# Attention core: value products on two column halves, and the softmax division moved behind them

## The chip, the cores and the metric

The kernel runs on one core of one Trainium2 chip. The metric is the time of one execution on the device, in microseconds (us). Engines are called as in the profile: PE is TensorE (matrix products), PEld its weight loads, DVE is VectorE, ACT is ScalarE, POOL is GpSimd, SP is SyncE, which issues the loads. PSUM is the memory that PE writes, in eight banks of 128 x 512 fp32 numbers.

## The reference

A two-layer backbone block: 512 tokens of width 1024 and 256 context tokens. Each layer is a half-step SwiGLU network, a token mixer and another half-step SwiGLU network, each with modulation and normalisation. The first layer's mixer is attention, and in it lies the change: 16 query heads of 64 on 4 key heads (four query heads share keys and values), blocks of 128 queries, each with the block's own keys, its neighbours' and all 256 context keys, and a logit ("sink") per head that only adds to the softmax's sum.

```
def block(bi):
    ...
    s_win = jnp.where(valid, s_win, NEG_INF)
    s_ctx = jnp.einsum('bqhgd,bkhd->bhgqk', q_b, kc, preferred_element_type=jnp.float32)
    sinks = jnp.broadcast_to(sink_logit, s_ctx.shape[:-1] + (1,))
    p = jax.nn.softmax(jnp.concatenate([s_win, s_ctx, sinks], axis=-1), axis=-1).astype(v.dtype)
    o = (jnp.einsum('bhgqk,bkhd->bqhgd', p[..., :SPAN], v_b)
         + jnp.einsum('bhgqk,bkhd->bqhgd', p[..., SPAN:SPAN + C_], vc))
    return o
```

## The kernel before

The large products (the two networks, the projections) run on PE with operands split into a rounded part and a rest (`wh`, `wl` for weights; three products instead of one). Weights come in tiles of 128 x 1024: loaded as `wr`, for some multiplied by a gate's row (`wr<-wr,gr`, on DVE), rounded on ACT (`wh`), and the rest taken on DVE (`wl<-wr,wh`).

The change lies in `attention`. Keys, values and queries are projected first (`group`, `kv_post`, `q_post`). Then follows the core: 16 steps, one per key head g and block b, in which four query heads (`GRP`) are handled at once. Blocks 0 and 3 have four key tiles of 128 (scores 512 wide, "narrow" below), blocks 1 and 2 have five (640 wide, "wide").

`scores` of a step: PE makes the scores of each head (s); DVE adds the mask, writes them to the tile p and takes the row's minimum of the negated scores (nm, in one or two instructions per head); ACT exponentiates p in place with the row's sum (sum) beside it. es is the exponential of the sink logit. At the end DVE adds es to sum, takes the reciprocal and scales p by it.

`weights_turned` of a step: PE turns the four p tiles into PSUM banks pt, one bank per key tile (16 or 20 turns), and ACT copies the banks to pT.

`values` of a step: one product per key tile, V as the stationary operand, the four heads' pT side by side as 512 columns. V holds each head's 64 columns twice, so o has the same values in rows 0 to 63 and 64 to 127; two ACT copies take the even heads from the upper half and the odd ones from the lower half into oT, which the output projection reads.

The loop over the steps writes the core out by hand: in step n stand `weights_turned` of n, `scores` of n + 2, in steps 3 to 6 a turn of queries (`q_flip`, qt), and `values` of n. In steps 2 to 5 DVE then splits queries (`q_parts`), in step 0 it adds a bias to the last ones (qb), and POOL rotates them (ra). In steps 7 to 11 one tile of the output projection's weights is prepared: wr at the step's start, wh and wl ahead of `values`. All engines but SP keep this order in the core (`pin`). PSUM tiles are taken from eight banks in turn.

Of the kernel before, what the change touches and what calls it, by code (L numbers as in the profile page):

```python
# [10 lines left out]
F32 = mybir.dt.float32  # L11
F32R = mybir.dt.float32r
AF = mybir.ActivationFunctionType
ALU = mybir.AluOpType

P = 128
# [13 lines left out]
KVH = 4  # L30
GRP = HEADS // KVH
HD = 64
# [11 lines left out]
HEAD_TURN = 2  # L44
HEAD_PE = 1
SLOTS = 42
EVAC_DVE = ()
CORE_FETCH = 7
CORE_TILES = 5
MOD_LAG = 3  # L50
# [52 lines left out]
class Emitter:  # L103
# [33 lines left out]
    def mm(self, out, lhsT, rhs, start, stop):  # L137
        self.nc.tensor.matmul(out, lhsT, rhs, start=start, stop=stop)
# [739 lines left out]
    def attention(self, w_kv, w_q, w_ao, h1, ch, rest):  # L878
        nc = self.nc
        ins = self.ins  # L880
        sync = nc.sync
        mm = self.mm
# [13 lines left out]
        V = []  # L896

        def kv_post(tp, ps):
            V.append(self.slot([P, 2, KVH, 2 * HD], F32, "V"))
            kv = self.slot([P, 2, 512], F32, "kvb")  # L900
            for tt in range(2):
                nc.vector.tensor_tensor(kv[:, tt], ps[:, tt * 512 : (tt + 1) * 512], bkv, ALU.add)
            kks = []
            for tt in range(2):
                t = 2 * tp + tt
                kr = kv[:, tt, :256]
                if t < NT:
                    kr = self.rope(kr, tabs[:, 0, t], tabs[:, 1, t], KVH, nc.vector)
                kk2 = self.slot([P, 2, KVH, 2, HD], F32, "kk2")
                k4 = kr.rearrange("p (h d) -> p h d", d=HD)  # L910
                for r in range(2):
                    nc.scalar.copy(kk2[:, 0, :, r].bitcast(F32R), k4)
                for r in range(2):
                    nc.vector.tensor_tensor(kk2[:, 1, :, r], k4, kk2[:, 0, :, r], ALU.subtract)
                kks.append(kk2)
            for tt in range(2):
                v4 = kv[:, tt, 256:512].rearrange("p (h d) -> p h d", d=HD).unsqueeze(2)
                nc.scalar.copy(
                    V[tp][:, tt].rearrange("p h (r d) -> p h r d", r=2), v4.broadcast_to([P, KVH, 2, HD])
                )  # L920
            return tp, kks

        def kv_flip(tp, kks, tt):
# [44 lines left out]
        def q_flip(tp, i, qb, q2s, tt):  # L968
            flip = self.bank2(nm="qt")
            for j in range(8):  # L970
                self.turn(flip[:, j * P : (j + 1) * P], q2s[tt][:, j].rearrange("p r d -> p (r d)"))
            q = self.slot([P, 8, P], F32R, "Q")
            for h in range(2):
                src = flip[:, h * BANK : (h + 1) * BANK].rearrange("p (j q) -> p j q", q=P)
                nc.scalar.copy(q[:, 4 * h : 4 * h + 4], src)
            Q[2 * tp + tt, i] = q
# [44 lines left out]
        sink = self.const([P, HEADS], F32, "sink")  # L1021
# [5 lines left out]
        oT = []  # L1027

        def scores(g, b):
            lo_t, hi_t = max(b - 1, 0), min(b + 1, NT - 1)  # L1030
            nw = (hi_t - lo_t + 1) * P
            win = [KX[g][:, part, lo_t * P : lo_t * P + nw] for part in range(2)]
            cx = [KC_[g // 2][:, g % 2, part] for part in range(2)]
            w_t = list(range(lo_t, hi_t + 1))
            c_t = list(range(NT, NT + NCT))
            segs = [(0, CTX, cx), (CTX, nw, win)] if b == NT - 1 else [(0, nw, win), (nw, CTX, cx)]
            keys = c_t + w_t if b == NT - 1 else w_t + c_t
            total = nw + CTX
            m0 = {0: 384, NT - 1: 0}.get(b, 256)
            cuts = [0, total] if total <= BANK else [0, nw, total]  # L1040
            part, nm, sm, es = (self.small([P, GRP], x) for x in ("part", "nm", "sum", "es"))
            s_l = [self.slot([P, total], F32, "p") for _ in range(GRP)]

            def expo(j):
                hd = g * GRP + j
                nc.scalar.activation(
                    s_l[j], s_l[j], AF.Exp, bias=nm[:, j : j + 1], scale=-1.0, accum_out=sm[:, j : j + 1]
                )
                if j % 2 == 1:
                    pair = slice(j - 1, j + 1)  # L1050
                    nc.vector.tensor_tensor(es[:, pair], sink[:, hd - 1 : hd + 1], nm[:, pair], ALU.add)
                    nc.scalar.activation(es[:, pair], es[:, pair], AF.Exp)

            for j in range(GRP):
                hd = g * GRP + j
                q = Q[b, hd // 8][:, hd % 8]
                least = nsink[:, hd : hd + 1]
                for c0, c1 in zip(cuts, cuts[1:]):
                    ps = self.bank("s")
                    for off, n, kp in segs:  # L1060
                        if c0 <= off < c1:
                            o = ps[:, off - c0 : off - c0 + n]
                            mm(o, q, kp[0], start=True, stop=False)
                            mm(o, q, kp[1], start=False, stop=True)
                    to = nm if c1 == total else part
                    nc.vector.tensor_tensor_reduce(
                        out=s_l[j][:, c0:c1], in0=ps[:, : c1 - c0], in1=mask[:, m0 + c0 : m0 + c1], scale=-1.0,
                        scalar=least, op0=ALU.add, op1=ALU.min, accum_out=to[:, j : j + 1],
                    )
                    least = to[:, j : j + 1]  # L1070
                if j > 0:
                    expo(j - 1)
            expo(GRP - 1)
            for j in range(0, GRP, 2):
                pair = slice(j, j + 2)
                nc.vector.tensor_tensor(sm[:, pair], sm[:, pair], es[:, pair], ALU.add)
                nc.vector.reciprocal(sm[:, pair], sm[:, pair])
                for i in range(j, j + 2):
                    nc.vector.tensor_scalar(s_l[i], s_l[i], sm[:, i : i + 1], None, ALU.mult)
            return g, b, keys, s_l  # L1080

        def weights_turned(g, b, keys, s_l):
            nk = len(keys)
            banks = [self.bank("pt") for _ in range(nk)]
            for i in range(nk):
                for j in range(GRP):
                    self.turn(banks[i][:, j * P : (j + 1) * P], s_l[j][:, i * P : (i + 1) * P])
            pT = []
            for i in range(nk):
                if i % 2 == 0:  # L1090
                    sb = self.slot([P, 2, 512], F32, "pT")
                src = banks[i]
                if i in EVAC_DVE:
                    nc.vector.tensor_copy(sb[:, i % 2], src)
                else:
                    nc.scalar.copy(sb[:, i % 2], src)
                pT.append(sb[:, i % 2])
            return g, b, keys, pT

        def values(g, b, keys, pT):  # L1100
            nk = len(keys)
            o = self.bank("o")
            for i, kt in enumerate(keys):
                mm(o, V[kt // 2][:, kt % 2, g], pT[i], start=(i == 0), stop=(i == nk - 1))
            tok = slice(b * P, (b + 1) * P)
            for r in range(2):
                rs = slice(r * HD, (r + 1) * HD)
                src = o[rs].rearrange("p (c r q) -> p c r q", c=2, r=2)[:, :, r]
                nc.scalar.copy(oT[g][rs, :, tok], src)

        steps = [(g, b) for g in range(KVH) for b in range(NT)]
        oT.append(self.slot([P, 2, SEQ], F32, "oT"))
# [2 lines left out]
        due = [scores(*steps[0])]  # L1115
        ps1 = group(1, w_q[1], between=lambda: due.append(scores(*steps[1])))
        q01 = q_bias(0, 1, ps0)
        for n, (g, b) in enumerate(steps):
            fetch = n >= CORE_FETCH and self.n_split < w_ao + CORE_TILES
            if fetch:  # L1120
                self.gate_next()
            t = weights_turned(*due.pop(0))
            if b == 0 and g > 0:
                oT.append(self.slot([P, 2, SEQ], F32, "oT"))
            if n + 2 < len(steps):
                due.append(scores(*steps[n + 2]))
            if Q_TURN <= n < Q_TURN + 4:
                q_flip(*(q01 if n < Q_TURN + 2 else q11), (n - Q_TURN) % 2)
            if fetch:
                self.weights(self.n_split, ahead=0)  # L1130
            values(*t)
            if n == 0:
                q11 = q_bias(1, 1, ps1)
                for i in range(4):
                    q_rope(*(q01 if i < 2 else q11), i % 2, nc.gpsimd)
            if Q_TURN - 1 <= n < Q_TURN + 3:
                q_parts(*(q01 if n < Q_TURN + 1 else q11), (n + 1 - Q_TURN) % 2)
# [205 lines left out]
```

## Time and profile before

| | |
|---|---|
| median of three runs | 2040.0 us (2038.52 to 2041.05) |
| the profiled execution | 2039.18 us, span 2037.3 us |
| PE busy | 2003.1 us, 98% of the span |
| DVE, ACT, POOL busy | 1324.4, 714.4, 50.5 us |
| granted TensorE clock | 0.998 of full speed |

Rows of groups read: line, engine, operation, out<-in by the program's names with buffer numbers left out, partitions x elements, count, then busy time in us and mean ns of one, and behind the second bar the engine's idle time just before them and who ended it. Nearly all lines are L70, a helper's, so groups are told apart by names. A product of fp32 tiles (o) leaves two records for each product of the program. Rows of the timeline read: start, duration, engine, operation. A duration includes the instruction's latency, so where instructions follow one another the distance between starts is what one costs.

### The profile page before, as it was taken

The numbers are of one execution on the slowest core, as the hardware profiler recorded it, in microseconds if no ns is written. First come the engines' busy times: TensorE is split into PE (matmuls) and PEld (weight loads), VectorE is DVE, ScalarE is ACT, GpSimd is POOL, SyncE is SP. The second block draws the span as 40 slices with busy tenths as digits, with TensorE's granted clock in tenths as the row PEclk, the third lists the DMA queues.
The fourth block names the chain that finished last, engine by engine and source line by source line (L and its number), as shares of the span: only waits on it lengthen the run. The fifth ranks groups of instructions, "written<-read, shape, count | busy, mean of one in ns | idle before, by whom it ended". The sixth has DMA issues, their size and how long they took to land.

```text
span 2037.3 us, 25228 instructions
## 1 busy us (share of the span) xinstructions
PE 2003.1 (98%) x9990; PEld 1683.6 (83%) x9990; DVE 1324.4 (65%) x1888; ACT 714.4 (35%) x1090; POOL 50.5 (2%) x56
## 2 busy tenths in 40 slices
PE   6999999999999999999999999999999999999998
PEld 5788888899888776888888889888888988888887
DVE  7659986598756887666657646665675882322854
ACT  3322233443634688422224323221332642222420
POOL 2000000000000300000000000000000000000000
PEclk9999999999999999999999999999999999999999
DMA  9656543387712002265543416454342223322321
GB/s 366 229 196 205 189 133 134 115 295 283 260 65 72 1 32 93 104 217 191 192 155 114 138 47 250 176 207 145 114 144 74 104 83 108 99 93 83 124 73 42
DMA packets 81910, 292.56 MB, mean 144 GB/s; under 512 B 9856, under 2 KB 10112, under 8 KB 81792
## 3 DMA queue, kind: packets, MB, share of 16 engines
q1 hardware_dynamic: 81792, 290.96, 41.4%
q8 instruction: 78, 1.28, 0.3%
q14 instruction: 40, 0.33, 0.0%
HBM read 288.83 MB, written 2.10 MB: 143 GB/s over the span
## 4 chain that ended last, share of the span: by engine, by line
PE 94%; DVE 4%; issue 0%; ACT 0%; DMA 0%; SPq 0%; DVEq 0%
PE up L70 52%; PE y L70 31%; PE qkv L70 4%; PE o L70 2%; DVE p L70 1%; DVE acc L70 1%; PE s L70 1%; PE pt L70 1%; PE tp L70 1%; PE f L70 1%; PE ab L70 0%; PE qt L70 0%; DVE wl L70 0%; DMA wr<-in_wi_head_dram 0%; PE gp L70 0%
## 5 line engine op out<-in xcount | busy, mean ns | idle before, releaser
L70 DVE TENSOR_TENSOR wl<-wr,wh 128x1024 fp32r<-128x1024 f32 x356 | 426.3, 1220 | 105.0 <-ACT wh L70 68.0
L70 ACT CAST wh<-wr 128x1024 fp32r<-128x1024 f32 (+1 forms) x364 | 367.3, 1046 | 191.7 <-PE y L70 99.7
L70 PE MATMUL up<-hh,wh 128*128 128x512 f32 (+1 forms) x1152 | 429.4, 373 | 0.0
L70 PE MATMUL up<-hl,wh 128*128 128x512 f32 (+1 forms) x1152 | 428.0, 372 | 0.0
L70 PE MATMUL up<-hh,wl 128*128 128x512 f32 (+1 forms) x1152 | 427.8, 371 | 0.0
L70 ACT ACTIVATE sg<-up 128x512 f32<-128x512 f32 (+1 forms) x110 | 61.2, 556 | 715.4 <-PE up L70 715.4
L70 PE MATMUL y<-wh,ul 128*128 128x512 f32 x920 | 302.5, 390 | 3.5 <-DVE ul L70 3.4
L70 PE MATMUL y<-wh,uh 128*128 128x512 f32 x920 | 303.2, 391 | 0.0
L70 PE MATMUL y<-wl,uh 128*128 128x512 f32 x920 | 302.3, 390 | 0.0
L70 DVE TENSOR_TENSOR u<-up,sg 128x512 f32<-128x512 f32 (+1 forms) x110 | 70.1, 637 | 354.1 <-PE up L70 353.8
L70 PEld LDWEIGHTS up<-hl,wh 128*128 128x128 f32 x1152 | 217.0, 188 | 37.6
L70 PEld LDWEIGHTS up<-hh,wl 128*128 128x128 f32 x1152 | 217.1, 188 | 37.1
L70 PEld LDWEIGHTS up<-hh,wh 128*128 128x128 f32 x1152 | 217.1, 188 | 36.9
L70 PEld LDWEIGHTS y<-wh,ul 128*128 128x128 f32 x920 | 173.1, 188 | 40.4 <-DVE ul L70 4.4
L70 PEld LDWEIGHTS y<-wh,uh 128*128 128x128 f32 x920 | 173.1, 188 | 35.9 <-ACT uh L70 0.4
L70 PEld LDWEIGHTS y<-wl,uh 128*128 128x128 f32 x920 | 173.1, 188 | 35.7
L70 DVE SCALAR_TENSOR_TENSOR acc<-mr,silu_c,acc 128x1024 f32<-128x1024 f32 x147 | 186.2, 1281 | 1.4
L70 DVE TENSOR_TENSOR wr<-wr,gr 128x1024 f32<-128x1024 f32 x104 | 124.8, 1221 | 29.4 <-DMA wr<-in_wo_dram 20.6
L70 PE MATMUL up<-h0h,wh 128*128 128x512 f32 x352 | 139.6, 397 | 3.3 <-ACT h0h L70 3.3
L70 PE MATMUL up<-h0h,wl 128*128 128x512 f32 x352 | 138.4, 393 | 0.0
L70 PE MATMUL up<-h0l,wh 128*128 128x512 f32 x352 | 138.2, 393 | 0.0
L70 DVE SCALAR_TENSOR_TENSOR x<-x,y 128x512 f32<-128x512 f32 x48 | 32.7, 682 | 105.3 <-PE y L70 105.3
(162 smaller groups left out, 2291.8 us busy)
## 6 DMA issues: line engine op xcount, KB each, us to landing
wr<-in_wi_dram SPq DMA_DIRECT2D x213, 512.0 KB, 4.5
mr<-in_mod_w_dram SPq DMA_DIRECT2D x144, 512.0 KB, 4.2
wr<-in_wo_dram SPq DMA_DIRECT2D x110, 512.0 KB, 3.6
m<-in_mod_head_dram SPq DMA_DIRECT2D x16, 512.0 KB, 8.2
wr<-in_wqkv_dram SPq DMA_DIRECT2D x12, 512.0 KB, 3.8
wr<-in_attn_wo_dram SPq DMA_DIRECT2D x8, 512.0 KB, 3.4
wr<-in_fourier_wo_dram SPq DMA_DIRECT2D x8, 512.0 KB, 3.6
wr<-in_wi_head_dram SPq DMA_DIRECT2D x8, 448.0 KB, 9.2
```

What stands on the lines that cost most here:

```text
L70: ins = f(*args, **kw)
```

## The change

V is stored once per head (64 columns). Each value product becomes two, for the even heads into rows 0 to 63 of o and for the odd ones into rows 64 to 127, with 256 columns each. p is no longer scaled. The four sums of a step get their reciprocals in one instruction that also spreads each over 64 elements (rs, 128 x 256); PE turns rs in two turns into a bank rr; ACT copies rr into oT's place, and DVE multiplies o by it there. es is made by one pair of instructions instead of two. The first pT bank of a step is copied by DVE instead of ACT (`EVAC_DVE`).

```diff
-EVAC_DVE = ()
+EVAC_DVE = (0,)
...
-            V.append(self.slot([P, 2, KVH, 2 * HD], F32, "V"))
+            V.append(self.slot([P, 2, KVH, HD], F32, "V"))
...
-                if j % 2 == 1:
-                    pair = slice(j - 1, j + 1)
-                    nc.vector.tensor_tensor(es[:, pair], sink[:, hd - 1 : hd + 1], nm[:, pair], ALU.add)
-                    nc.scalar.activation(es[:, pair], es[:, pair], AF.Exp)
...
+            nc.vector.tensor_tensor(es, sink[:, g * GRP : (g + 1) * GRP], nm, ALU.add)
             expo(GRP - 1)
-            for j in range(0, GRP, 2):
-                pair = slice(j, j + 2)
-                nc.vector.tensor_tensor(sm[:, pair], sm[:, pair], es[:, pair], ALU.add)
-                nc.vector.reciprocal(sm[:, pair], sm[:, pair])
-                for i in range(j, j + 2):
-                    nc.vector.tensor_scalar(s_l[i], s_l[i], sm[:, i : i + 1], None, ALU.mult)
-            return g, b, keys, s_l
+            nc.scalar.activation(es, es, AF.Exp)
+            return g, b, keys, s_l, sm, es
...
+            nc.vector.tensor_tensor(sm, sm, es, ALU.add)
+            rs = self.pool.tile([P, GRP, HD], F32, tag="rs", name=self.name("rs"), bufs=2)
+            nc.vector.reciprocal(rs, sm.unsqueeze(2).broadcast_to([P, GRP, HD]))
             nk = len(keys)
...
+            rows = self.bank("rr")
+            for c in range(2):
+                self.turn(rows[:, c * P : (c + 1) * P], rs[:, 2 * c : 2 * c + 2].rearrange("p r d -> p (r d)"))
             pT = []
...
+            nc.scalar.copy(oT[g][:, :, b * P : (b + 1) * P], rows[:, : 2 * P].rearrange("p (c q) -> p c q", c=2))
             return g, b, keys, pT
...
-            o = self.bank("o")
+            o = self.bank("o")[:, : 2 * P].rearrange("p (c q) -> p c q", c=2)
             for i, kt in enumerate(keys):
-                mm(o, V[kt // 2][:, kt % 2, g], pT[i], start=(i == 0), stop=(i == nk - 1))
+                heads = pT[i].rearrange("p (c r q) -> p c r q", c=2, r=2)
+                for r in range(2):
+                    mm(
+                        o[r * HD : (r + 1) * HD], V[kt // 2][:, kt % 2, g], heads[:, :, r],
+                        start=(i == 0), stop=(i == nk - 1),
+                    )
             tok = slice(b * P, (b + 1) * P)
-            for r in range(2):
-                rs = slice(r * HD, (r + 1) * HD)
-                src = o[rs].rearrange("p (c r q) -> p c r q", c=2, r=2)[:, :, r]
-                nc.scalar.copy(oT[g][rs, :, tok], src)
+            nc.vector.tensor_tensor(oT[g][:, :, tok], o, oT[g][:, :, tok], ALU.mult)
```

The order on DVE around the weight fetch of step 7, before: es of the last head pair, then the two halves of sums, reciprocals and scalings, then the fetch's two instructions, then the next scores' first mask (ISA).

```order
 L70 TENSOR_TENSOR es_6536<-sink,nm_6534 128x2
 L70 TENSOR_TENSOR sum_6535<-sum_6535,es_6536 128x2
 L70 RECIPROCAL sum_6535<-sum_6535 128x2
 L70 TENSOR_SCALAR p_6537<-p_6537,sum_6535 128x640
 L70 TENSOR_SCALAR p_6538<-p_6538,sum_6535 128x640
 L70 TENSOR_TENSOR sum_6535<-sum_6535,es_6536 128x2
 L70 RECIPROCAL sum_6535<-sum_6535 128x2
 L70 TENSOR_SCALAR p_6539<-p_6539,sum_6535 128x640
 L70 TENSOR_SCALAR p_6540<-p_6540,sum_6535 128x640
 L70 TENSOR_TENSOR wl_6592<-wr_5505,wh_6591 128x1024
 L70 TENSOR_TENSOR wr_5517<-wr_5517,gr_4995 128x1024
 L70 ISA p_6634,part_6630<-s_6638,mask_5555,nsink 128x384
```

The same place after the change:

```order
 L70 TENSOR_TENSOR es_6527<-sink,nm_6525 128x4
 L70 TENSOR_TENSOR wl_6573<-wr_5505,wh_6572 128x1024
 L70 TENSOR_TENSOR oT_6175<-o_6576,oT_6175 128x2x128
 L70 TENSOR_TENSOR wr_5517<-wr_5517,gr_4995 128x1024
 L70 TENSOR_TENSOR sum_6429<-sum_6429,es_6430 128x4
 L70 RECIPROCAL rs_6589<-sum_6429 128x256
 L70 COPY pT_6614<-pt_6591 128x512
 L70 ISA p_6625,part_6621<-s_6629,mask_5555,nsink 128x384
```

wl now follows es directly, the product with o and the gate multiply stand between it and sum, and sum and reciprocal are those of the step before, ahead of the eviction and the next masks.

On PE, the end of step 0 and the start of step 1, before: the last scores, the value products of step 0 (the number behind a row counts the program's products), the first turns of step 1.

```order
 L70 MATMUL s_5857<-K_843_5010,Q_5598 128x384 x2
 L70 MATMUL s_5861<-KC_847_5014,Q_5598 128x256 x2
 L70 MATMUL o_5877<-pT_5815,V_5066 128x512 x2
 L70 MATMUL o_5877<-pT_5818,V_5323 128x512 x2
 L70 MATMUL pt_5907<-ident,p_5716 128x128
```

After the change, the same value products, and then the end of step 1's turns:

```order
 L70 MATMUL s_5842<-K_843_5010,Q_5598 128x384 x2
 L70 MATMUL s_5846<-KC_847_5014,Q_5598 128x256 x2
 L70 MATMUL o_5854<-pT_5801,V_5066 64x256 x4
 L70 MATMUL o_5854<-pT_5804,V_5323 64x256 x4
 L70 MATMUL pt_5890<-ident,p_5706 128x128
...
 L70 MATMUL pt_5894<-ident,p_5709 128x128
 L70 MATMUL rr_5915<-ident,rs_5888 128x128 x2
 L70 MATMUL s_5935<-KC_847_5014,Q_5635 128x256 x2
```

There are twice as many products of half the columns, and two turns of rs stand between the turns of p and the next scores. In steps 10 and 11 two gate multiplies of the output projection's weights come to stand between DVE's sum and reciprocal.

More of the change, by code (lines that the diff above doesn't have):

```diff
@@ L916, in kv_post @@
             for tt in range(2):
[L917 to L920, printed above, removed]
+                nc.scalar.copy(V[tp][:, tt], kv[:, tt, 256:512].rearrange("p (h d) -> p h d", d=HD))
             return tp, kks
@@ L1044, in expo @@
             def expo(j):
-                hd = g * GRP + j
                 nc.scalar.activation(
@@ L1072, in scores, with weights_turned @@
                     expo(j - 1)
+            nc.vector.tensor_tensor(es, sink[:, g * GRP : (g + 1) * GRP], nm, ALU.add)
             expo(GRP - 1)
-            for j in range(0, GRP, 2):
-                pair = slice(j, j + 2)
-                nc.vector.tensor_tensor(sm[:, pair], sm[:, pair], es[:, pair], ALU.add)
-                nc.vector.reciprocal(sm[:, pair], sm[:, pair])
-                for i in range(j, j + 2):
-                    nc.vector.tensor_scalar(s_l[i], s_l[i], sm[:, i : i + 1], None, ALU.mult)
-            return g, b, keys, s_l
-        def weights_turned(g, b, keys, s_l):
+            nc.scalar.activation(es, es, AF.Exp)
+            return g, b, keys, s_l, sm, es
+        def weights_turned(g, b, keys, s_l, sm, es):
+            nc.vector.tensor_tensor(sm, sm, es, ALU.add)
+            rs = self.pool.tile([P, GRP, HD], F32, tag="rs", name=self.name("rs"), bufs=2)
+            nc.vector.reciprocal(rs, sm.unsqueeze(2).broadcast_to([P, GRP, HD]))
             nk = len(keys)
@@ L1121, in attention @@
                 self.gate_next()
-            t = weights_turned(*due.pop(0))
             if b == 0 and g > 0:
                 oT.append(self.slot([P, 2, SEQ], F32, "oT"))
+            t = weights_turned(*due.pop(0))
             if n + 2 < len(steps):
```

## The prediction

> **What bounds the kernel now.** I read the page first, of it the chain that ended last.
>
> ```profile
> PE 94%; DVE 4%; issue 0%; ACT 0%; DMA 0%; SPq 0%; DVEq 0%
> ```
>
> TensorE is the bound almost everywhere, so time won or lost on TensorE's path inside the attention core arrives at the end unchanged. The core runs from the first turn of softmax weights (pt) to the last value product (o). The timeline of PE gives both ends, the table by stage what is busy between (behind the length stand the busy times of PE, PEld, DVE, ACT and POOL with their counts, then the granted clock).
>
> ```profile
> 676.28 1.91 PE L70 MATMUL pt<-ident,p 128*128 128x128 f32 x16
> ...
> 806.62 3.60 PE L70 MATMUL o<-pT,V 128*128 128x512 f32 x8
> ```
>
> ```profile
> 676.00:811.00 135.00, 131.12 (x694) 92.67 (x693) 111.97 (x338) 106.81 (x259) 16.05 (x16) 1.00 0.12 40
> ```
>
> The core takes 810.22 - 676.28 = 133.9 us at full clock. PE is busy for 131 of 135 us and DVE for 112: a change that makes PE lighter meets DVE soon. The chain in order of time gives the lengths of PE's parts, the by-form groups a product record's mean duration.
>
> ```profile
> 690.60 4.29 PE o L70 x10
> 694.89 2.18 PE pt L70 x20
> 697.08 1.92 PE s L70 x16
> 698.99 4.29 PE o L70 x10
> 703.29 1.75 PE pt L70 x16
> 705.03 2.38 PE s L70 x16
> 707.41 0.87 PE qt L70 x8
> ```
>
> ```profile
> L70 PE MATMUL o<-pT,V 128*128 128x512 f32 x144 | 64.8, 595 | 0.5 <-DVE part L70 0.4
> ```
>
> A product of one key tile is two records of 0.429 us, so five key tiles take 4.29 and four 3.43; a turn takes 0.109. Steps whose new scores are 512 wide (narrow) spend 1.92 us on scores, those of 640 (wide) 2.38. A turn of q takes 0.87.
>
> **The change, part by part.** *Value products.* Each product of 512 columns becomes two of 256, one into array columns 0 to 63 and one into 64 to 127. One after the other they stream what they did. If the halves stream at once it is half of that, plus one record of 0.11 that finds no partner: 2.25 for five key tiles and 1.82 for four. No row has two products side by side; these are the bounds. I take half, since the two touch other columns and other PSUM partitions and neither waits for the other. A switch between full-width and half-width work can cost nothing, or at most the tail that a record has behind its stream, 0.595 - 0.429 = 0.17; twice a step that is 0 to 5.4 us in all. I take nothing and keep 5.4 for the range. [...]
>
> *Two turns of the reciprocals (rr)* stand on PE between the pt turns and the next scores: 0.22 us a step, and PE waits there for DVE.
>
> *DVE* loses four scalings, one sum, one reciprocal and one es a step; it gains a product, an eviction of a PSUM bank and a reciprocal of 256 elements. Its timeline in a step with a weight fetch, with PE's row ahead of it and ACT's behind it, and two rows of a narrow step:
>
> ```profile
> 740.15 0.60 PE L70 MATMUL s<-K,Q 128*128 128x384 f32 x2
> ...
> 740.78 0.62 DVE L70 CUSTOM_DVE_ANT_0 p<-s,mask,nsink 128x384 f32<-128x384 f32 x1 [2.15 <-PE s L70]
> ...
> 745.68 0.16 DVE L70 TENSOR_TENSOR es<-sink,nm 128x2 f32<-128x2 f32 x1
> 745.76 0.16 DVE L70 TENSOR_TENSOR sum<-sum,es 128x2 f32<-128x2 f32 x1
> 745.95 0.17 DVE L70 RECIPROCAL sum<-sum 128x2 f32<-128x2 f32 x1
> 746.15 1.02 DVE L70 TENSOR_SCALAR p<-p,sum 128x640 f32<-128x640 f32 x2
> ...
> 748.40 1.22 DVE L70 TENSOR_TENSOR wl<-wr,wh 128x1024 fp32r<-128x1024 f32 x1
> 749.54 1.22 DVE L70 TENSOR_TENSOR wr<-wr,gr 128x1024 f32<-128x1024 f32 x1
> 750.67 0.61 DVE L70 CUSTOM_DVE_ANT_0 p<-s,mask,nsink 128x384 f32<-128x384 f32 x1
> ...
> 751.85 0.62 DVE L70 CUSTOM_DVE_ANT_0 p<-s,mask,nsink 128x384 f32<-128x384 f32 x1
> ```
>
> ```profile
> 745.68 0.83 ACT L70 ACTIVATE p<-p,nm 128x640 f32<-128x640 f32 x1 [0.16 <-DVE nm L70]
> ...
> 747.54 0.74 ACT L70 COPY oT<-o 64x256 f32<-64x256 f32 x2
> ```
>
> ```profile
> 760.56 0.74 DVE L70 CUSTOM_DVE_ANT_0 p<-s,mask,nsink 128x512 f32<-128x512 f32 x1
> 761.23 0.08 DVE L70 DVE_READ_ACCUMULATOR2_ANT nm<- 128x1 f32 x1
> ```
>
> From the first score to its mask it is 0.63. Masks take 1.18 a head when wide (750.67 to 751.85), 0.67 when narrow. es is put at 0.12 with its wait, sum at 0.19, each weight instruction at 1.14. On ACT the last exponential starts 0.16 after the last mask, and 1.86 later it, es and wh are done. So wl can start 2.0 us after the masks. Today two sums, two reciprocals and four scalings (745.76 to 748.40) fill this time. After the change wl stands right behind es, and DVE waits 1.9 us. Queued behind wl are the product, the gate multiply wr, sum and the reciprocal, for which PE's rr waits, and the next scores wait behind rr.
>
> The prices of the new DVE instructions come from these groups and rows:
>
> ```profile
> L70 DVE RECIPROCAL sum<-sum 128x2 f32<-128x2 f32 x10 | 1.7, 166 | 0.3
> L70 DVE TENSOR_TENSOR sum<-sum,es 128x2 f32<-128x2 f32 x10 | 1.5, 154 | 0.0
> ```
>
> ```profile
> L70 DVE TENSOR_TENSOR u<-up,sg 128x256 f32<-128x256 f32 x22 | 9.3, 422 | 13.6 <-PE up L70 13.4
> ```
>
> ```profile
> 688.04 1.28 DVE L70 TENSOR_TENSOR qb<-qkv,bq 128x512 f32<-128x512 f32 x2
> ...
> 703.13 0.42 DVE L70 CAST q<-ra 128x512 fp32r<-128x512 f32 x1
> 703.59 0.69 DVE L70 TENSOR_TENSOR q<-ra,q 128x512 f32<-128x512 f32 x1
> ```
>
> The product, with one operand in PSUM, is 0.42. The eviction of 128x512 is 0.42 (a cast in SBUF) to 0.64 (a bias add out of PSUM). It lies beside rr and the first scores (0.22 + 0.63 = 0.85), so it costs nothing; without that cover it would cost up to 0.64 a step, 10 us.
>
> The reciprocal R decides. Priced like a tensor_tensor of 256 it is 0.4. But with two elements it takes 12 ns more than the sum, 6 ns an element; if that holds for each, R = 0.4 + 256 x 0.006 = 1.9. A fixed 12 ns fits two elements as well. I take 1.9, because the row compared with has the same tile, size and source memory, and a longer pass for each element is the plainer reading; 0.4 stays as the other end. [...]
>
> *The rest.* ACT loses an es, one pT eviction and one of two oT copies; it isn't the bound. V's copies ahead of the core shrink beside the projection. No DMA and nothing of POOL's queue is added or moved.
>
> **The sum**, as loops from one rr to the next. Wide (7 steps) goes through DVE: rr 0.22, first mask 0.63, masks 4.72, es 0.12, product 0.42, sum 0.19, R: 6.30 + R = 8.20. Narrow (7 steps, all with five key tiles) goes through PE, then DVE: 0.22 + 1.92 + 2.25, the product's tail 0.2, 0.42, 0.19, R: 5.20 + R = 7.10 (PE alone 2.18 + 0.22 + 1.92 + 2.25 = 6.57). Together 107.1. The start (q bias 1.28, sum, R, less what had begun) is 2.9, the last two steps 7.2: 117.2. To these come DVE instructions ahead of the reciprocal: four splits of q (1.05 each) and a q bias, 5.5; five fetches at 1.14 + 1.14 + 1.9, 20.9, less 0.9 in each of two narrow ones, which go through DVE alone (4.26 + R); and two gate multiplies of the projection, which the order has between sum and reciprocal in the two steps after, 2.3. The whole is 144.1 against 133.9: +10.2.
>
> The profiled execution took 2039.2 us, 0.8 under the median of the three runs. So 2049.4 by this execution and 2050 by the median. Behind the core nothing changes but that it starts later.
>
> **The rivals.** *The reciprocal is cheap* (R = 0.4), the one mechanism that ends on the other side. Wide is then 6.70, and narrow PE's 6.57. With start, end and bias that makes 102.1, q's splits and turns 4.0, fetches 16.0 (three wide waits and wl 3.0, two gate multiplies 1.1, two narrow 2.3), the two later gate multiplies 2.3: 124.4, or -9.5, and 2030. For it: a fixed 12 ns. The two ends of R move the core by 19.7 us, so the sign turns near R = 1.1.
>
> *The halves don't stream at once*, so that the change doesn't do on PE what its layout is for. With R = 1.9: five narrow loops +2.04, four wide ones that now go through PE +0.5 (two with q's turns 0.9 more), the last two steps +3.6: +17.6, and 2068. With R = 0.4 PE's own work is the loop again (8.6 narrow, 7.8 to 8.2 wide) but for fetches: 141 us, or +7, and 2047. For it: no two records in the rows are spaced closer than what they stream.
>
> **How the numbers follow.** Halves at once and R near 1.9: 0.42 (2050; own range 2043 to 2058, from R 1.5 to 2.15 and switches of 0 to 5.4). Cheap reciprocal: 0.29 (2030 to 2035). Serial and dear: 0.15 (2068). Serial and cheap: 0.08 (2047). R near 1.1, level: 0.06. A measurement of this kernel tells 0.2% (4 us) from no change. The last case and 0.01 of the others are the same; faster 0.29, slower 0.64. The range goes from the cheap case, 2030, to just short of the serial dear one, 2066; it leaves out 0.05 below and 0.12 above.
>
> **What would show it.** A RECIPROCAL of 128x256 at 1.9 us or at 0.4 settles the main step. Value records of 64x256 at a spacing of 0.11 on average, or 0.21, settle the second. wl should have some 9 us of idle time before it, ended by ACT's wh, and PE's rr some 0.5 us a narrow step, ended by DVE; the core should span near 144 us. I am wrong if the reciprocal lies between 0.6 and 1.2, if PE doesn't wait at rr, or if scores wait for PSUM banks, of which the core takes one more a step out of eight.

## The result, and the profile after

The changed kernel takes 2057.5 us (median of four runs, 2055.6 to 2058.0), the kernel before in the same job 2040.5 (2038.5 to 2041.1). The ratio is 1.0088, with an interval of 1.0075 to 1.0100. The change makes the kernel slower by 0.9%. The profiled execution spans 2055.8 us, 18.5 more than before.

First the chain that ended last, as on the page of before; then the core's stretch, from the first turn (pt) to the last value product, in the table by stage with the same columns.

```profile
PE 91%; DVE 6%; DMA 2%; ACT 1%; issue 1%; SPq 0%; DVEq 0%; ACTq 0%
```

```profile
676.60:828.10 151.50, 117.47 (x865) 96.67 (x863) 115.23 (x270) 92.67 (x214) 15.62 (x16) 0.90 0.10 34
```

The core has grown from 133.9 to 151 us, which is nearly the whole difference. PE does some 13 us less work in it, 117 instead of 131, and nevertheless waits 34 us ahead of rr (row below). DVE has 68 instructions fewer (270 for 338) and some 3 us more to do. The granted clock, 1.00 before, is 0.90. The groups of the core by shape show what became of the terms:

```profile
L70 PE MATMUL o<-pT,V 128*64 128x256 f32 x288 | 35.5, 392 | 0.1
L70 DVE RECIPROCAL rs<-sum 128x256 f32<-128x256 f32 x16 | 28.0, 1752 | 0.5
L70 PE MATMUL rr<-ident,rs 128*128 128x128 f32 x32 | 7.7, 327 | 33.6 <-DVE rs L70 33.5
L70 DVE TENSOR_TENSOR wl<-wr,wh 128x1024 fp32r<-128x1024 f32 x6 | 7.4, 1225 | 10.4 <-ACT wh L70 10.4
L70 DVE TENSOR_TENSOR oT<-o,oT 128x256 f32<-128x256 f32 x16 | 6.8, 422 | 9.6 <-PE o L70 7.6 <-ACT p L70 2.0
```

The value products fell from 64.8 to 35.5 us. The reciprocal of 256 elements takes 1752 ns, against 166 for two. PE waits 33.5 us for it, in front of rr. DVE in turn waits 10.4 us for ACT's wh and 9.6 ahead of the product with o.

DVE's timeline in step 7's weight fetch is the place of which the prediction showed the rows before; PE's rows of the same time stand behind it.

```profile
747.79 0.17 DVE L70 TENSOR_TENSOR es<-sink,nm 128x4 f32<-128x4 f32 x1
749.78 1.23 DVE L70 TENSOR_TENSOR wl<-wr,wh 128x1024 fp32r<-128x1024 f32 x1 [1.82 <-ACT wh L70]
750.92 0.42 DVE L70 TENSOR_TENSOR oT<-o,oT 128x256 f32<-128x256 f32 x1
751.25 1.22 DVE L70 TENSOR_TENSOR wr<-wr,gr 128x1024 f32<-128x1024 f32 x1
752.39 0.16 DVE L70 TENSOR_TENSOR sum<-sum,es 128x4 f32<-128x4 f32 x1
752.58 1.75 DVE L70 RECIPROCAL rs<-sum 128x256 f32<-128x256 f32 x1
754.25 0.63 DVE L70 COPY pT<-pt 128x512 f32<-128x512 f32 x1
755.75 0.62 DVE L70 CUSTOM_DVE_ANT_0 p<-s,mask,nsink 128x384 f32<-128x384 f32 x1 [0.88 <-PE s L70]
```

```profile
746.39 1.97 PE L70 MATMUL pt<-ident,p 128*128 128x128 f32 x16
754.39 0.69 PE L70 MATMUL rr<-ident,rs 128*128 128x128 f32 x2 [6.03 <-DVE rs L70]
754.73 0.99 PE L70 MATMUL s<-K,Q 128*128 128x384 f32 x2
755.51 0.63 PE L70 MATMUL s<-KC,Q 128*128 128x256 f32 x2
755.94 0.84 PE L70 MATMUL s<-K,Q 128*128 128x384 f32 x2
...
757.57 0.40 PE L70 MATMUL s<-KC,Q 128*128 128x256 f32 x2
757.81 0.52 PE L70 MATMUL s<-K,Q 128*128 128x384 f32 x2
```

Between es and sum (752.39) nothing on DVE serves the rr for which PE waits: DVE waits 1.82 for wh, then come wl, the product and wr. All of PE's idle time in the core, 33.7 us (151.2 less 117.5), lies ahead of an rr to within 0.1, so scores didn't wait for PSUM banks, which the prediction had named as a sign of being wrong. PE has finished its turns by 748.4 and stands until 754.39. When it goes on, its first scores are slow: a pair of 256 columns takes 0.43 from start to start (755.51 to 755.94), where later it takes 0.24 (757.57 to 757.81). The table by stage has the granted clock of the two stretches:

```profile
754.39:757.50 3.11, 3.11 (x12) 3.11 (x13) 2.09 (x7) 0.82 (x2) 0.00 (x0) 0.50 0.00 0
757.50:758.00 0.50, 0.50 (x6) 0.50 (x5) 0.35 (x3) 0.47 (x2) 0.00 (x0) 1.00 0.00 0
```

### The profile page after: what moved, and what is told of

Same layout as the page of the kernel before. It is cut to its first block, busy times and chain, and to the rows that moved or that the text cites. A ratio compares the mean times of both kernels' runs of the same rounds, so it can differ in the third digit from the quotient of the medians.

```text
span 2055.8 us, 25445 instructions
## 1 busy us (share of the span) xinstructions
PE 1991.3 (97%) x10166; PEld 1689.8 (82%) x10166; DVE 1327.0 (65%) x1808; ACT 698.7 (34%) x1042; POOL 50.1 (2%) x56
## 4 chain that ended last, share of the span: by engine, by line
PE 91%; DVE 6%; DMA 2%; ACT 1%; issue 1%; SPq 0%; DVEq 0%; ACTq 0%
PE up L70 52%; PE y L70 30%; PE qkv L70 4%; DVE p L70 1%; DVE rs L70 1%; PE s L70 1%; PE tp L70 1%; DVE acc L70 1%; DMA xt<-in_xT_dram 1%; PE o L70 1%; ACT p L70 1%; PE f L70 1%; DMA wr<-in_wi_head_dram 0%; DVE wl L70 0%; PE ab L70 0%
```

## The experiments

The kernel before measured 2039.3 us beside the first four, 2039.5 beside the others. All ratios are to it.

**A reciprocal on the four sums alone.** The long reciprocal becomes one of four elements and a copy that spreads them.

```diff
-            nc.vector.reciprocal(rs, sm.unsqueeze(2).broadcast_to([P, GRP, HD]))
+            nc.vector.reciprocal(sm, sm)
+            nc.vector.tensor_copy(rs, sm.unsqueeze(2).broadcast_to([P, GRP, HD]))
```

> The changed kernel, with the reciprocal taken of the four sums and a copy that spreads them over 128x256. Theory (the long reciprocal sits on the loop from one rr to the next): 1.67 us of DVE become about 0.2 + 0.35, so 1.1 us less in each of 15 loops, less some 2 us where narrow steps then meet PE's own 6.6 us: 2042 to 2044 us, idle time before rr down from 33 us to under 20. Rival (the loss comes from PE: half-width products, their mode changes, one PSUM bank more): 2055 to 2058 us.

Measured: 2040.2 us (2038.1 to 2041.8), ratio 1.0005 (0.9995 to 1.0014), 17 us less than the change and some 2 less than the theory's range. Groups of its core:

```profile
L70 DVE RECIPROCAL sum<-sum 128x4 f32<-128x4 f32 x16 | 2.8, 177 | 0.5
L70 DVE COPY rs<-sum 128x256 f32<-128x256 f32 x16 | 5.5, 345 | 0.6
L70 PE MATMUL rr<-ident,rs 128*128 128x128 f32 x32 | 7.0, 302 | 19.5 <-DVE rs L70 19.4
```

The pair costs about 0.5 us instead of 1.75, and PE's wait before rr falls from 33.5 to 19.4. So in this place of DVE's order the reciprocal's length is enough to account for the slowdown. It is not all that stands in front of rr, though: with a cheap reciprocal the kernel is level, not faster.

**The halves one after the other.** The loop over the halves goes outside the loop over key tiles.

```diff
-            for i, kt in enumerate(keys):
-                heads = pT[i].rearrange("p (c r q) -> p c r q", c=2, r=2)
-                for r in range(2):
+            for r in range(2):
+                for i, kt in enumerate(keys):
+                    heads = pT[i].rearrange("p (c r q) -> p c r q", c=2, r=2)
```

> The changed kernel, with all products of the even heads ahead of all of the odd heads, so that neighbours in the queue use the same array columns. Theory (the halves stream at once only when neighbours differ in columns): records at 0.21 instead of 0.116 us, +1.6 to 2.0 us a step, on the loop in narrow steps and in the last two, part of it covered in wide ones: 2070 to 2077 us. Rival (a 64-column product is quick by itself): records stay at 0.12, 2057 us.

Measured: 2065.4 us (2064.4 to 2065.7), ratio 1.0127 (1.0112 to 1.0142): slower than the change, by less than expected. Two rows of its PE timeline:

```profile
700.21 3.72 PE L70 MATMUL o<-pT,V 128*64 128x256 f32 x20
711.09 2.86 PE L70 MATMUL o<-pT,V 128*64 128x256 f32 x16
```

If the records of one half follow each other at 0.214 (half of what a 512-column record took before), then (20 - 3) x 0.214 = 3.64 and (16 - 3) x 0.214 = 2.78 come within 0.08 of the rows. By this sum, an estimate from the two rows, some three records still overlap, and the rest run singly; the rows differ by 0.86 for four records, 0.215 each. In the change, with the halves alternating, two records start 0.007 apart and the next two 0.21 later (718.38 and on), and 16 records take 1.95 us (a row further below): they do stream two at once.

**wl later.** wl moves on DVE from ahead of the product to behind the next step's first eviction; everything else is the change's.

```diff
             t = weights_turned(*due.pop(0))
+            if late:
+                hi, lo, raw = late.pop()
+                nc.vector.tensor_tensor(lo, raw, hi.bitcast(F32), ALU.subtract)
...
-                self.weights(self.n_split, ahead=0)
+                j = self.n_split
...
+                nc.scalar.copy(hi, raw)
+                late.append((hi, lo, raw))
```

> The changed kernel, with the fetch's wl moved on DVE from behind es to behind the next step's reciprocal and pT eviction; ACT's wh stays. Theory (DVE waits 1.8 us for ACT's wh in each of five fetches, at the head of the queue to rr): the idle time of 10 us before wl goes, and the core is 9 to 11 us shorter: 2047 to 2049 us. Rival (wl's wait is covered by the wait for o or by PE): under 3 us.

Measured: 2041.9 us (2040.7 to 2046.0), ratio 1.0013 (1.0004 to 1.0023). That is 15.6 less than the change, where 8.5 to 10.5 was expected. Its DVE timeline at the new place:

```profile
750.97 0.63 DVE L70 COPY pT<-pt 128x512 f32<-128x512 f32 x1
751.51 1.21 DVE L70 TENSOR_TENSOR wl<-wr,wh 128x1024 fp32r<-128x1024 f32 x1
752.64 0.61 DVE L70 CUSTOM_DVE_ANT_0 p<-s,mask,nsink 128x384 f32<-128x384 f32 x1
```

I had counted the wait for wh alone. But wl's own 1.14 now lies where DVE waited 0.88 for the first scores, and the clock between 738 and 810 rose from 0.81 to 0.95. These two are read from the rows; no run separates them.

**The half products without the division moved.** The kernel before, with V once, the products on two halves and one copy of o; sums, reciprocals and scalings as before.

```diff
...
+                heads = pT[i].rearrange("p (c r q) -> p c r q", c=2, r=2)
+                for r in range(2):
+                    mm(
+                        o[r * HD : (r + 1) * HD], V[kt // 2][:, kt % 2, g], heads[:, :, r],
+                        start=(i == 0), stop=(i == nk - 1),
+                    )
+            nc.scalar.copy(oT[g][:, :, b * P : (b + 1) * P], o)
```

> The kernel before, with V once and the two half-width products alone; the scaling stays where it was, and one ACT copy takes o. Theory (the halves win on PE, and the division's new place loses it): PE's value products 29 us shorter, DVE with 111 us busy then sets the core at 118 to 125 us instead of 134: 2025 to 2032 us. Rival (half-width products bring nothing by themselves because of mode changes): 2038 to 2042 us.

Measured: 2029.2 us (2028.5 to 2030.0), ratio 0.9951 (0.9936 to 0.9966). Its core in the table by stage:

```profile
676.74:800.45 123.71, 110.90 (x833) 86.09 (x831) 109.95 (x337) 98.84 (x243) 16.06 (x16) 0.97 0.12 40
```

The halves alone save 10 us, though PE's value products got 29 shorter. DVE, busy for 110 of 124 us, is now as full as PE, and the chain that ended last runs through DVE's masks, scalings and weight instructions for most of the core. The moved division was a way to relieve DVE; as ordered, it did the opposite.

**The division moved, without the half products.**

```diff
...
-            V.append(self.slot([P, 2, KVH, HD], F32, "V"))
+            V.append(self.slot([P, 2, KVH, 2 * HD], F32, "V"))
...
+                mm(o, V[kt // 2][:, kt % 2, g], pT[i], start=(i == 0), stop=(i == nk - 1))
...
+            for r in range(2):
+                h = slice(r * HD, (r + 1) * HD)
+                src = o[h].rearrange("p (c r q) -> p c r q", c=2, r=2)[:, :, r]
+                nc.vector.tensor_tensor(oT[g][h, :, tok], src, oT[g][h, :, tok], ALU.mult)
```

> The change with V stored twice and the value products 512 wide again (two records of 0.429 a key tile); the division stays behind the products, and DVE needs two multiplications of 64 rows for it instead of one, a row of 0.42 more a step. Theory (the long reciprocal stands in DVE's loop from one rr to the next; the half-width products are a gain of about 11 us, as the kernel with these alone showed): 2057.5 + the value products' share that lies on the loop. In the ten or so loops that go from rr through scores, products and the reciprocal the full products add 1.82 to 2.04 each and the second multiplication 0.4 in all 16: 2057.5 + 18 to 20 + 6 = 2075 to 2085, with rr's idle time above 33.5. Rival (the division is free once the products are full width, because PE then hides the reciprocal): within 3 us of the kernel before, 2037 to 2043.

Measured: 2086.2 us (2085.9 to 2087.5), ratio 1.0232 (1.0216 to 1.0247), just above the theory's range and far from the rival. In the kernel before, the halves are worth 10.0 us (2039.3 less 2029.2). Here the difference is 28.6 (2086.2 less 2057.5), but the kernels also differ in the second multiplication on DVE. The two take 0.86 together where the change's one takes 0.42, so up to 7 us in 16 steps are the multiplication's, and the halves' share is about 22 or more. That is twice what they bring in the kernel before: in 11 of the 16 steps DVE waits for o here (29.3 us in all), so that PE's products and DVE's product, sum and reciprocal take turns, and what either takes lies on the path.

**The reciprocal one place earlier.** Sum and the long reciprocal of the next step stand ahead of this step's wl and product; nothing gets shorter. `recips` holds the change's two instructions.

```diff
+        def recips(g, b, keys, s_l, sm, es):
...
             if n + 2 < len(steps):
                 due.append(scores(*steps[n + 2]))
+            if due:
+                due[0] = recips(*due[0])
```

> The changed kernel with one move: sum and the long reciprocal of step n + 1 stand on DVE ahead of step n's product instead of behind it. Theory (in narrow steps DVE waits 1.6 to 2.6 us for the value products; the reciprocal of 1.67 fits into that wait; in wide and fetch steps DVE is the loop and only the order changes): narrow loops shorten by up to 1 us each, 2050 to 2054. Rival (the product, now behind the reciprocal, lets the o banks come free later and the loop doesn't shorten): 2056 to 2060.

Measured: 2030.8 us (2030.6 to 2031.5), ratio 0.9959 (0.9944 to 0.9974). That is 26.7 less than the change where I had expected 4 to 7: a clear miss. DVE's timeline in step 7's fetch, the one shown above:

```profile
737.35 0.16 DVE L70 TENSOR_TENSOR es<-sink,nm 128x4 f32<-128x4 f32 x1
737.43 0.15 DVE L70 TENSOR_TENSOR sum<-sum,es 128x4 f32<-128x4 f32 x1
737.62 1.75 DVE L70 RECIPROCAL rs<-sum 128x256 f32<-128x256 f32 x1
739.34 1.23 DVE L70 TENSOR_TENSOR wl<-wr,wh 128x1024 fp32r<-128x1024 f32 x1
740.48 0.42 DVE L70 TENSOR_TENSOR oT<-o,oT 128x256 f32<-128x256 f32 x1
740.81 1.21 DVE L70 TENSOR_TENSOR wr<-wr,gr 128x1024 f32<-128x1024 f32 x1
741.95 0.68 DVE L70 COPY pT<-pt 128x512 f32<-128x512 f32 x1
742.55 0.61 DVE L70 CUSTOM_DVE_ANT_0 p<-s,mask,nsink 128x384 f32<-128x384 f32 x1
```

I had allowed for the wait for o in narrow steps alone. But the reciprocal also fills the wait for wh: es to the next mask is 5.2 us here, 8.0 in the change. And wl, the product and wr, which rr doesn't need, no longer stand in front of it; they run while PE makes the next scores. The rival's mechanism, an o bank that comes free later, shows once, ahead of step 1's rr, for 1.2 us. The five loops of steps 7 to 11 take 44.7 us instead of 61.5. With a reciprocal as dear as the change's (1.75), the kernel is faster than the one before.

**PE kept busy.** Dummy products of `ident` and p, written into the unused half of the rr bank, fill most of PE's wait in steps 8 to 12.

```diff
             rows = self.bank("rr")
+            for _ in range({8: 12, 9: 9, 10: 5, 11: 9, 12: 8}.get(g * NT + b, 0)):
+                mm(rows[:, 2 * P :], self.ident, s_l[0][:, : 2 * P], start=True, stop=True)
```

> The changed kernel with dummy products (ident x p, 256 columns, into the unused half of the rr bank) on PE ahead of rr in steps 8 to 12, 12, 9, 5, 9 and 8 of them, which fill most of PE's wait for the reciprocals there. Theory (the granted clock of 0.74 to 0.87 in these steps follows from PE's waits of several us, and costs about 2 to 3 us of the core because the first scores after a wait run at a slower clock): the clock between 738 and 810 near 1.0 and 2054 to 2056. Rival (the slower clock costs nothing that DVE's loop doesn't hide): clock near 1.0 and 2056 to 2059. Third (the clock isn't set by these waits): clock stays near 0.8.

Measured: 2053.8 us (2053.6 to 2054.1), ratio 1.0072 (1.0057 to 1.0087). Beside the change's 1.0088 the intervals overlap, so the timing alone doesn't show the gain; the traces do. The spans are 2052.1 and 2055.8, and the cores run within 0.1 us of each other up to the first dummy product. The stretches from one rr to the next of steps 8, 12 and 13 in the change, and of steps 8 and 12 here:

```profile
754.39:767.17 12.78, 8.38 (x54) 7.18 (x55) 9.43 (x24) 7.03 (x15) 0.00 (x0) 0.88 0.13 41
803.29:812.81 9.52, 9.39 (x54) 7.99 (x55) 7.16 (x22) 5.49 (x13) 0.00 (x0) 0.72 0.00 1
812.81:820.01 7.20, 6.99 (x59) 5.70 (x59) 6.32 (x18) 5.50 (x16) 0.00 (x0) 1.00 0.23 74
```

```profile
754.30:766.54 12.24, 10.89 (x72) 9.13 (x73) 9.43 (x24) 7.03 (x15) 0.00 (x0) 1.00 0.15 44
800.45:809.09 8.64, 8.52 (x54) 7.14 (x55) 7.16 (x22) 5.55 (x13) 0.00 (x0) 0.80 0.01 3
```

With PE kept busy the clock stays at 1.00 and step 8 is 0.54 us shorter, though PE does more. Step 12 has no dummy products of its own behind its rr; its clock is 0.80 instead of 0.72, and it is 0.88 shorter. Thus the slower clock follows from the waits and costs time.

**All eviction by ACT again** (`EVAC_DVE = ()`, else the change).

> The changed kernel with all pT banks copied by ACT again, as before the change, and nothing else different. Theory (DVE's eviction of 0.63 lies beside rr and the first scores, so it costs nothing; ACT has time for it): 2056 to 2059, no difference from the changed kernel. Rival (the eviction delays DVE's masks in most steps): up to 0.63 in each of 16 steps, 2047 to 2056. Second rival (ACT's later first bank delays the value products): 2059 to 2063.

Measured: 2056.2 us (2055.8 to 2056.4), ratio 1.0080 (1.0063 to 1.0097), as the theory had it. It can't be told from the change: DVE's eviction costs next to nothing there.

**Everything late moved.** Short reciprocal with copy, placed early; wl and wr behind the next step's turns; all evictions by ACT.

```diff
-EVAC_DVE = (0,)
+EVAC_DVE = ()
...
+            nc.vector.reciprocal(sm, sm)
+            nc.vector.tensor_copy(rs, sm.unsqueeze(2).broadcast_to([P, GRP, HD]))
...
+            if late:
+                hi, lo, raw = late.pop()
+                nc.vector.tensor_tensor(lo, raw, hi.bitcast(F32), ALU.subtract)
+            if fetch:
+                self.gate_next()
...
+            if due:
+                due[0] = recips(*due[0])
```

> The changed kernel with all of DVE's late work moved: first pT bank copied by ACT again; reciprocal on the four sums alone and a copy that spreads them; sums and reciprocals of step n + 1 ahead of step n's product; wl and the gate multiply behind the next step's turns. Theory (what the change lost is only the order and the length of the work on DVE between the scores and rr): PE goes back to being the loop, the core is 110 to 120 us against 151.5, the rr idle time under 8 us, and the time 2015 to 2026, below both kernels and below the half products alone (2029). Rival (turns of rr, the added DVE product and ACT's evictions cost the rest whatever the order): no better than the half products alone, 2029 to 2040.

Measured: 2021.8 us (2020.0 to 2022.3), ratio 0.9913 (0.9897 to 0.9930), the fastest of all. Its core, and its rr:

```profile
675.88:789.80 113.92, 109.67 (x865) 87.74 (x863) 85.58 (x269) 96.81 (x229) 15.75 (x16) 1.00 0.13 40
```

```profile
L70 PE MATMUL rr<-ident,rs 128*128 128x128 f32 x32 | 6.4, 282 | 2.4 <-DVE rs L70 2.1 <-DVE oT L70 0.2
```

PE is busy for 110 of 114 us, at full clock, and waits 2.4 us at rr. DVE is down to 86. So the change's parts are good ones, and their order and the form of the reciprocal were what made it slow.

The same kernel with DVE evicting the first bank (`EVAC_DVE = (0,)`):

> The kernel with all of DVE's late work moved (2021.8), with the first pT bank copied by DVE as in the change. DVE is busy 86 of 114 us of the core there, PE 110, so PE is the loop. Theory (DVE has room for 10 us more): 2020 to 2024, no difference. Rival (in the wide and the fetch steps, where DVE has a weight tile and five masks, the eviction lies on the loop): 0.63 in some six to ten steps, 2025 to 2029.

Measured: 2022.7 us (2020.5 to 2023.4), ratio 0.9914 (0.9899 to 0.9928). No difference: there is room on DVE for it.

## Why the prediction was right, and where its sum was not

2050 was predicted and 2057.5 came, slower as forecast. By steps:

- **The reciprocal**, the step on which the sign hung, came out as taken: 1.75 us, or 6.2 ns an element ((1752 - 166) / 254), where the dear end said 1.9 from 6 ns an element on top of 0.4. The rows of before couldn't tell this price from a fixed 12 ns, as the prediction said; that it took the dear end was a judgement on one difference between two rows, and it held. From its start to PE's rr it is 1.81 (752.58 to 754.39). The ends of the range taken for it, 1.5 and 2.15, were the author's estimate: no run shows either, and the 16 reciprocals of the change average 1752 ns.
- **The halves stream at once**, as taken. The switches between full and half width (the "mode changes" of two expectations), put at nothing, cost about 0.16 a step, 2.6 us in 16 steps: 0.06 out of half width, as 16 records and the switch take 1.88 (717.90 to 719.78, below) where 1.82 was predicted, and 0.10 into it, as a turn of queries ahead of the products takes 0.97 (716.93 to 717.90) where it took 0.87 before. What these 0.06 and 0.10 consist of, no run shows.

```profile
716.93 1.03 PE L70 MATMUL qt<-ident,q 128*128 128x128 f32 x8
717.90 1.95 PE L70 MATMUL o<-pT,V 128*64 128x256 f32 x16
719.78 2.40 PE L70 MATMUL pt<-ident,p 128*128 128x128 f32 x20
```

- **wl's wait** was put at some 9 us; it is 10.4. **The eviction at nothing**: the runs agree (2056.2 us with ACT's alone, 2057.5 with DVE's).
- **PE's wait at rr**, put at 0.5 us for a plain narrow step, is 0.2 where step 13's loop ends (820.01, below). Of the 33.5 us in all, 21.7 stand ahead of the rr of steps 8 to 12, behind the five fetches.
- **The core** was put at 144.1 us and took 151.2. Here the sum failed. The table sets the prediction's terms, each put to the loop in which it stands, against the distances between rr's starts (the first and last of the 15 rows used, from PE's timeline of the change):

```profile
678.34 0.38 PE L70 MATMUL rr<-ident,rs 128*128 128x128 f32 x2
...
820.01 0.41 PE L70 MATMUL rr<-ident,rs 128*128 128x128 f32 x2 [0.21 <-DVE rs L70]
```

| loop of step | terms | predicted | change | PE kept busy |
|---|---|---|---|---|
| 0 | wide, q bias | 9.48 | 9.94 | |
| 1 | narrow | 7.10 | 8.69 | |
| 2 | narrow, split of q | 8.15 | 8.23 | |
| 3, 4 | wide, split | 9.25 each | 9.10, 9.23 | |
| 5 | narrow, split | 8.15 | 9.12 | |
| 6 | narrow, wr | 8.24 | 9.17 | |
| 7 | wide, fetch | 12.38 | 12.57 | 12.57 |
| 8 | wide, fetch | 12.38 | 12.78 | 12.24 |
| 9 | narrow, fetch | 10.38 | 11.08 | 10.37 |
| 10 | narrow, fetch, one gate multiply more | 11.52 | 12.41 | 11.42 |
| 11 | wide, fetch, the other in wr's place | 12.38 | 12.63 | 12.12 |
| 12 | wide | 8.20 | 9.52 | 8.64 |
| 13 | narrow | 7.10 | 7.20 | |
| sum | | 134.0 | 141.7 | |

Two terms were missing. First, the turn of queries, 0.87 us of PE: the prediction counted it in both rivals and left it out of its own narrow loops 5 and 6, which go through PE. They are 1.9 us longer than predicted, of which the two turns are 1.7. Second, the clock. The sum took PE at full clock throughout, and the loops 1 and 8 to 12 ran at 0.72 to 0.88. They are 5.2 us longer than predicted (loop 7's half clock, from 750.66 to its end, falls into PE's wait alone). Where the dummy products hold the clock up, loops 8 to 11 come within 0.3 us of the prediction's terms: what it said of their work was right. For loop 1 no run kept PE busy ahead of it; that its excess of 1.6 is the clock too (0.80, behind a wait of 2.97) is read from the trace alone, in which PE works for 3.41 us of this loop at half clock (a row in the last section), which is 1.7 us of work lost. In the narrow loops the switches' 0.16 and the reciprocal, 0.09 shorter up to rr than the 1.90 taken, nearly cancel. Start and end together were 0.6 us shorter than said, and loop 0's excess of 0.5 stays open.

The cheap reciprocal's rival came out 10 us too low: it promised 2030, and a short reciprocal gave 2040, with 19.4 us of waits at rr and a clock of 0.91 between 738 and 810. In the change's order the sign would have turned near a price of 0.5, at which the kernel is level, not 1.1. And the prediction saw that sum and reciprocal stand last in DVE's row, behind wl, the product and wr; it priced them there, and didn't see that the place cost more than the length: moving them gave 26.7 us, shortening them 17.3.

## What to carry to other kernels

When an engine's result is awaited by the bound engine, put it first in its engine's queue, ahead of work that nobody waits for and of instructions that themselves wait for a third engine; here that was worth more (26.7 us) than making it three times shorter (17.3). Where an operation's time grew with its elements as the reciprocal's did here (177 ns for 4, 1752 for 256), do it on the fewest elements and spread the result with a copy (345 ns). The halves took 29 us off PE and brought 10, as DVE had no room: change the bound engine and the next one together. And add to a sum of waits what the slower clock behind them costs (5.2 us in six loops here).

## What the runs showed of the hardware

A reciprocal on DVE took 166 ns for 2 elements a partition (before), 177 for 4 (the reciprocal on the four sums alone) and 1752 for 256 (the change). The copy that spreads four values over 256 elements took 345 ns.

In the core of the change TensorE's granted clock was 1.00 or 0.50 and switched twelve times; it was 0.50 for 3.41 or 6.83 us at a time, each time in or behind a wait of PE. The table by stage, cut at the first five switches and at the last three:

```profile
689.22:692.63 3.41, 3.41 (x18) 2.81 (x18) 3.19 (x9) 2.56 (x7) 3.41 (x4) 0.50 0.00 0
692.63:750.66 58.03, 47.70 (x388) 39.07 (x386) 44.96 (x113) 39.57 (x96) 1.54 (x2) 1.00 0.06 19
750.66:757.48 6.82, 3.09 (x12) 3.10 (x13) 5.76 (x12) 1.34 (x4) 0.00 (x0) 0.50 0.00 0
757.48:767.73 10.25, 5.85 (x49) 4.65 (x48) 7.85 (x19) 6.32 (x15) 0.00 (x0) 1.00 0.17 51
...
795.03:801.86 6.83, 4.15 (x35) 2.95 (x33) 4.74 (x12) 4.75 (x11) 0.00 (x0) 1.00 0.00 0
801.86:808.69 6.83, 5.40 (x22) 4.99 (x24) 5.51 (x15) 2.60 (x6) 0.00 (x0) 0.50 0.00 0
```

The lengths are 1, 17, 2 and 3 times 3.41 us, and 2 and 2 times; the switches not shown lie on the same steps. So in this core all switches lay on a grid of 3.41 us, whatever the moments at which PE stopped or started. The clock fell in the wait or up to 0.9 us after it (688.28 to 689.22), some 1.6 us after it with the reciprocal earlier (776.45 to 778.02), and came back while PE worked.

In the core of the change PE was idle for 2.03 to 2.86 of the 3.41 us in the six stretches of the grid after which the clock fell from 1.00, and for at most 1.71 in those after which it stayed there. Waits of 2.10 (PE kept busy), 2.61 (the change), 2.80 (reciprocal earlier) and 2.97 (the change) were followed by the slow clock. The length of a wait alone doesn't tell: with the division moved alone, scores of 256 columns started 0.24 apart behind a wait of 1.96 (rr at 738.87) and 0.43 apart behind one of 1.97 (rr at 750.52), and with the halves alone they started 0.43 apart behind a wait of 1.63 (779.65 to 780.08), 0.24 later on (785.70 to 785.94). In the change 0.24 went with a clock of 1.00 and 0.43 with 0.50. What is counted in a stretch stays open.

Half-width products that alternate between the two halves ran two at once: in the change two records started 0.007 us apart, the next two 0.21 later, and 16 took 1.95. With one half wholly ahead of the other 16 took 2.86, of which by the sum above only some three overlapped and the rest took some 0.215 each: here the order of issue decided.
